# The down half of an MLP in 2x2 block products for two of three token groups

## The chip, the cores and the metric

One Trainium2 chip, one of its cores. The metric is the device time of one execution in microseconds; lower is better. The engines are PE (matrix products; PEld is its weight load), DVE (VectorE), ACT (ScalarE), POOL (GpSimd) and SP (SyncE), which here issues every data transfer.

## The reference, cut to what matters

Two layers over 1152 tokens (1024 of a prompt, 8 streams with 16 new ones each), model width 1024, inner width 4096:

```python
for l in range(DEPTH):                       # DEPTH = 2
    x = x + merge(attention parts of rmsnorm(x, norm1[l])) @ w_out[l]
    x = x + jnp.square(jax.nn.relu(rmsnorm(x, norm2[l]) @ w_up[l])) @ w_down[l]
y = rmsnorm(x, final_norm)
```

Everything is float32. The change is in the second line of the loop: `u = relu(h @ w_up)^2`, a matrix of 4096 by 1152, and `u @ w_down`.

## The kernel before, in words

**Layout and precision.** Activations lie feature by token: a tile has 128 features on the partitions and G = 384 tokens along the row, so there are NG = 3 token groups. A float32 operand is split in two halves of the type fp32r, a rounded value H (ACT) and the remainder L (`sub_l`, DVE or POOL). A product of two such operands is three matmuls: H by H, H by L, L by H. Each matmul is 128x128 weights against 128x384 values.

**Up stage.** For i from 0 to 15, two chunks (128 rows each) of `u` are made. `up_plain(i)` makes them directly: 3 groups, 2 chunks, 8 chunks of depth, 3 matmuls each. From i = 2, `up_seven(i)` (L1323) takes groups 0 and 1 as the two columns of a 2x2 block product: the weights' blocks are a11, a12, a21, a22 (two chunks of `u` by two halves of the depth), and seven block products in place of eight give the four results. The sums of weight blocks s1 to s4 are made for each i (L1328, L1329 on POOL, L1330, L1331 on DVE) and split again (`w_pair`, L1295: ACT copy, then DVE subtraction); the sums t1 to t4 of the activations were made once by `t_prep` (L1275) and stay in SBUF. The third group is done directly beside the seven products (`third`, L1339) for i below 14; for i = 14 and 15 it follows behind, in `up_plain(14, (2,))` and `up_plain(15, (2,))`. `put_u` (L1308) takes a result out of PSUM, squares it and stores it to DRAM.

**Down stage.** 8 blocks b of 4 chunks of `u` (512 rows). `load_u` (L1375) loads the 12 tiles of a block back and splits each in H (L154, ACT) and L (L138, DVE); they lie in the pool `h`, 48 slots of 128x384, which also holds the split input of the up stage. `down_block` (L1410) loops over 8 output chunks m: every second m it loads and splits 512 KB of weights (`w_raw`, `w_pair`), then, for each group, 4 chunks of depth by 3 matmuls run into one PSUM bank, and one DVE addition (L1424) adds it to `x`. The last block runs group after group, its weights loaded again for each, so that a group's final norm can start early.

**Order.** The program is traced in the order of the source and a list scheduler of the framework orders each engine's queue by priority and its own estimate of times; each engine then runs its queue in order and waits on semaphores. A tile of a pool takes a slot when an earlier tile of that pool is released by its last reader. SP's queue, too, runs in order: a transfer that waits for its slot or for its data holds what is queued behind it. The raw weight tiles `wr` have 2 slots, the split ones `wh`/`wl` 2 in one pool and every third pair in another.

Of the kernel before, what the change touches and what calls it, by code (L numbers as in the profile page):

```python
# [40 lines left out]
def body(ctx, tc, t):  # L41
# [84 lines left out]
    lmask = cpool.tile([P, 6, 64], F32, name="lmask")  # L126
    smask = cpool.tile([P, N_STREAM], F32, name="smask")
    fnorm = cpool.tile([P, KD], F32, name="fnorm")
    rm = cpool.tile([P, G + P], F32, name="rm")
    GP.memset(rm, 1.0)  # L130
    GP.memset(rm[:, 0:G].rearrange("p (n s) -> p n s", s=64)[:, :, 0:1], 0.0)
    GP.memset(rm[:, G:G + P].rearrange("p (n s) -> p n s", s=16)[:, :, 0:1], 0.0)
    cqbd = cpool.tile([P, N_STREAM, 32], F32, name="cqbd")
    GP.memset(cqbd.rearrange("p s k -> p (s k)"), 0.0)
# [5 lines left out]
    wextra, wturn = [None], [0]  # L140

# [57 lines left out]
    def norm_group(xs, gains, hs, g, pool=SQ_POOL):  # L199
        r = inv_rms([x[:, gsl(g)] for x in xs], 1024.0, pool=pool)  # L200
        for c in range(KD):
            hs[c].append((hpc("hH"), hpc("hL")))
            f = piece("hf")
            V.scalar_tensor_tensor(f, xs[c][:, gsl(g)], gains[:, c:c + 1], r, ALU.mult, ALU.mult)
            copy(hs[c][g][0], f)
            sub_l(V if c % 2 else GP, hs[c][g][1], f, hs[c][g][0])
        return r

    def raw_group(xs, gains, hs, g):

        for c in range(KD):
            hs[c].append((hpc("hH"), hpc("hL")))
            x = xs[c][:, gsl(g)]
            copy(hs[c][g][0], x, scale=gains[:, c:c + 1])
            V.scalar_tensor_tensor(hs[c][g][1], x, gains[:, c:c + 1], hs[c][g][0].bitcast(F32), ALU.mult, ALU.subtract)

# [17 lines left out]
    xs = [xpool.tile([P, NT], F32, name=nm("x")) for _ in range(KD)]  # L234
# [9 lines left out]
    for g in range(NG):  # L244
        for c in range(KD):
            load(xs[c][:, gsl(g)], t["x"][:, c, gsl(g)])
# [7 lines left out]
    load(lmask, t["lmask"])  # L254
# [3 lines left out]
    for l in range(DEPTH):  # L258
# [92 lines left out]
        if l > 0:  # L351
            for c in range(KD):
                store(t["xspill"][:, c, :], xs[c])
# [3 lines left out]
            ws = [load_first(l, i) for i in range(3)]  # L357
        def first_put(i, g, o):
# [211 lines left out]
        def ca_head(c, h, ap):  # L570
# [3 lines left out]
            for g in range(NG):  # L574
                lo, hi = g * G, min(NP_, (g + 1) * G)
                w = hi - lo
                for ci in (C_CQ, C_CK):
# [3 lines left out]
                    if ci == C_CQ:  # L581
                        copy(qH[:, lo:hi], f[:, 0:w])
                        sub_l(GP, qL[:, lo:hi], f[:, 0:w], qH[:, lo:hi])
                        if g == 2:
                            GP.tensor_copy(cqbd[hr, :, 16 * h:16 * h + 16],
# [25 lines left out]
        def ca_scores(c, box):  # L611
# [3 lines left out]
            for s0 in range(0, N_STREAM, 3):  # L615
                n = min(3, N_STREAM - s0)
                pt = bank("pv", "cass")
                for j in range(n):
                    mm(pt[r3, j * 144:(j + 1) * 144], cqbd[:, s0 + j, :], c.kc[:, s0 + j, :], start=True, stop=True)
# [94 lines left out]
        def gla_prep(p, g, gp):  # L714
# [20 lines left out]
            V.tensor_tensor_scan(u.b, rm[:, P:P + G] if g == 2 else rm[:, 0:G], la, 0.0, ALU.mult, ALU.add)  # L735
# [17 lines left out]
        def gla_levels(u, gp, mq):  # L753
            g = u.g
            for li, s in enumerate(LEVELS):
# [23 lines left out]
                mk = lmask[:, None, li, :].bitcast(U32).rearrange("p j (n s) -> p j n s", s=s)  # L779
# [97 lines left out]
        def gla_stream():  # L877
            with ExitStack() as stack:
                yield from gla_units(open_pool(stack, "gla"))
# [320 lines left out]
        def ca_stage():  # L1200
            with ExitStack() as outer:
                op = open_pool(outer, "cao")
                box = dict(scs=op.tile([96, N_STREAM, 144], F32, name=nm("scs")),
# [20 lines left out]
        xs = [xpool.tile([P, NT], F32, name=nm("x")) for _ in range(KD)]  # L1224
        banks(d=4, tp=2, pv=2)

        def out_last(gs):

            for m in range(KD):
                for g in gs:  # L1230
# [6 lines left out]
                    V.tensor_tensor(xs[m][:, gsl(g)], o, xo, ALU.add)  # L1237
# [23 lines left out]
        for g in range(NG):  # L1261
            with tc.high_priority(offset=100):
                raw_group(xs, gains, hs, g)
                rs.append(up.tile([P, G], F32, name=nm("rs")))
                copy(rs[g], inv_rms([x[:, gsl(g)] for x in xs], 1024.0))
                for c in range(KD):
                    store(t["xmid"][:, c, gsl(g)], xs[c][:, gsl(g)])
# [4 lines left out]
        def u_tile(s):  # L1272
            return up.tile([P, G], F32, tag="u", name=nm(s), bufs=5)

        def t_prep(j):  # L1275
            fs = []
            for c in (j, j + KH):
                for g in range(2):
                    f = tpool.tile([P, G], F32, tag="f", name=nm("f"), bufs=4)
# [3 lines left out]
            f11, f12, f21, f22 = fs  # L1283
# [5 lines left out]
            for n, f in ((2, t2), (3, t3), (1, t1), (4, t4)):  # L1289
# [3 lines left out]
                ts[n].append(o)  # L1293

# [13 lines left out]
        def put_u(ci, g, z):  # L1308
# [14 lines left out]
        def up_seven(i, rest):  # L1323
            raw = [w_raw(t["w_up"][l, 2 * i + c]) for c in range(2)]
            a11, a12, a21, a22 = (raw[x][:, y * KH:(y + 1) * KH, :] for x in range(2) for y in range(2))
            sa, sb = (tpool.tile([P, KD, P], F32, tag="ws", name=nm("ws"), bufs=2) for _ in range(2))
# [4 lines left out]
            V.tensor_tensor(s4, a12, s2, ALU.subtract)  # L1331

            def prod(o, w, half, x, first):
                for j in range(KH):
                    for k, (wi, ri) in enumerate(((0, 0), (0, 1), (1, 0))):
                        mm(o, w[wi][:, half * KH + j, :], x[j][ri], start=first and j == k == 0,
                           stop=j == KH - 1 and k == 2, skip_group_check=True)
# [21 lines left out]
            put_u(2 * i, 0, X)  # L1359
# [7 lines left out]
            put_u(2 * i + 1, 1, add("z22", Z, ec))  # L1367
# [3 lines left out]
            put_u(2 * i + 1, 0, add("z21", W, eb))  # L1371
            prod(Z, ws, 1, h2[1], False)
            put_u(2 * i, 1, add("z12", Z, eb))

        def load_u(b, pool, n):  # L1375
            us = []
            for q in range(4):
                row = []
                for g in range(NG):
# [187 lines left out]
```

## Time and profile before

| | |
|---|---|
| median of 3 runs | 3208.78 us (3202.6 to 3211.04) |
| the profiled execution | 3202.21 us, span 3200.4 us |
| granted TensorE clock, mean | 0.977 |
| busy share of the span | PE 95%, PEld 91%, DVE 62%, ACT 43%, POOL 25% |
| moved by DMA | 358.10 MB, mean 112 GB/s |

From the timeline of layer 0: the part with attention ends near 853 us, the up stage runs to about 1204 us, the down stage to about 1603 us; in layer 1 the same points lie at 2433, 2780 and 3187 us. A window's row gives its length, then each engine's busy time with the number of its instructions in brackets, then the granted clock, the share of DMA time and the rate in GB/s. A row of a group of instructions gives line, engine, operation, output and inputs, count, then busy time and the mean of one in ns, then the idle time ahead of it and what ended that.

### The profile page before, as it was taken

The numbers are of one execution on the slowest core, as the hardware profiler recorded it, in microseconds if no ns is written. First come the engines' busy times: TensorE is split into PE (matmuls) and PEld (weight loads), VectorE is DVE, ScalarE is ACT, GpSimd is POOL, SyncE is SP. The second block draws the span as 40 slices with busy tenths as digits, with TensorE's granted clock in tenths as the row PEclk, the third lists the DMA queues.
The fourth block names the chain that finished last, engine by engine and source line by source line (L and its number), as shares of the span: only waits on it lengthen the run. The fifth ranks groups of instructions, "written<-read, shape, count | busy, mean of one in ns | idle before, by whom it ended". The sixth has DMA issues, their size and how long they took to land.

```text
span 3200.4 us, 50248 instructions
## 1 busy us (share of the span) xinstructions
PE 3041.5 (95%) x18172; PEld 2911.2 (91%) x18172; DVE 1974.7 (62%) x3903; ACT 1371.0 (43%) x2995; POOL 811.4 (25%) x1010
## 2 busy tenths in 40 slices
PE   7999999988999999999999999989989999999998
PEld 7888887877999999999989898878879999999998
DVE  4665497885755565545555656978866555644446
ACT  4554354775533342212245544557754333412213
POOL 4332356552301110000153313554522111000002
PEclk9999899998999999999999999999999999999999
DMA  5333215224523245322343322142353223633313
GB/s 177 107 110 103 91 50 162 67 85 148 166 93 102 95 156 167 104 72 89 113 154 119 104 82 91 55 154 78 96 175 125 99 97 100 216 99 95 106 55 119
DMA packets 221144, 358.10 MB, mean 112 GB/s; under 512 B 27072, under 2 KB 185504, under 8 KB 220896
## 3 DMA queue, kind: packets, MB, share of 16 engines
q1 hardware_dynamic: 220896, 354.90, 34.6%
q8 instruction: 143, 2.34, 0.3%
q14 instruction: 105, 0.86, 0.1%
HBM read 251.77 MB, written 103.02 MB: 111 GB/s over the span
## 4 chain that ended last, share of the span: by engine, by line
PE 74%; DVE 11%; ACT 5%; DMA 4%; issue 3%; POOL 1%; SPq 1%; DVEq 0%; ACTq 0%; POOLq 0%
PE z L56 61%; PE pv L56 3%; PE s L56 2%; PE ptp L71 2%; DMA wr<-in_w_up_dram 1%; DMA cf<-zs_dram 1%; ACT P L427 1%; PE lev L56 1%; PE glao L56 1%; DVE ng L422 1%; SPq L74 1%; DVE ga L780 1%; PE rb L56 1%; DVE sbd L833 1%; DVE mq L771 1%
## 5 line engine op out<-in xcount | busy, mean ns | idle before, releaser
L56 PE MATMUL z<-uH,wdn 128*128 128x384 f32 x3072 | 781.7, 334 | 0.0
L56 PEld LDWEIGHTS z<-uH,wdn 128*128 128x128 f32 x3072 | 554.4, 188 | 0.0
L56 PE MATMUL z<-uL,wdn 128*128 128x384 f32 x1536 | 513.5, 334 | 0.0
L56 PE MATMUL z<-hH,wup 128*128 128x384 f32 x1728 | 451.8, 336 | 6.9 <-DVE u L1311 5.5
L1424 DVE TENSOR_TENSOR x<-z,x 128x384 f32<-128x384 f32 x336 | 186.9, 556 | 315.8 <-PE z L56 314.5
L56 PEld LDWEIGHTS z<-hH,wup 128*128 128x128 f32 x1728 | 314.7, 189 | 9.1 <-DVE u L1311 6.1
L1299 ACT ACTIVATE wdn<-wr 128x1024 fp32r<-128x1024 f32 x80 | 84.7, 1059 | 487.4 <-PE z L56 483.8
L56 PE MATMUL z<-hL,wup 128*128 128x384 f32 x864 | 290.4, 336 | 0.0
L56 PEld LDWEIGHTS z<-uL,wdn 128*128 128x128 f32 x1536 | 288.3, 188 | 0.0
L169 POOL TENSOR_TENSOR sq<-x 128x384 f32<-128x384 f32 x28 | 29.6, 1058 | 894.9 <-DVE x L1424 797.9
L1312 ACT ACTIVATE u<-u 128x384 f32<-128x384 f32 x192 | 100.0, 521 | 280.3 <-DVE u L1311 276.3
L1311 DVE SCALAR_TENSOR_TENSOR u<-z,rs 128x384 f32<-128x384 f32 x192 | 106.5, 555 | 156.9 <-PE z L56 155.0
L427 ACT ACTIVATE P<-s,ng 128x320 f32<-128x320 f32 (+5 forms) x288 | 157.7, 552 | 99.9 <-DVE ng L424 63.5
L1328 POOL TENSOR_TENSOR ws<-wr 128x512 f32<-128x512 f32 x28 | 46.3, 1653 | 537.7 <-DMA wr<-in_w_up_dram 440.2
L56 PE MATMUL z<-ts,wus 128*128 128x384 f32 x1008 | 180.5, 335 | 0.8 <-ACT wus L1299 0.8
L138 DVE TENSOR_TENSOR PT<-ptp,PT 128x512 fp32r<-128x512 f32 (+3 forms) x288 | 146.4, 516 | 52.9 <-ACT PT L154 44.6
L154 ACT ACTIVATE PT<-ptp 128x512 fp32r<-128x512 f32 (+3 forms) x288 | 128.6, 461 | 115.3 <-PE ptp L71 114.1
L56 PEld LDWEIGHTS z<-ts,wus 128*128 128x128 f32 x1008 | 174.9, 188 | 1.6 <-ACT wus L1299 1.4
L56 PEld LDWEIGHTS z<-hL,wup 128*128 128x128 f32 x864 | 163.2, 189 | 0.0
L71 PE MATMUL ptp<-ident,P 128*128 128x128 f32 x792 | 140.3, 282 | 18.4 <-DVE PT L138 6.8
L422 DVE TENSOR_REDUCE ng<-s 128x1 f32<-128x320 f32 (+5 forms) x288 | 146.5, 515 | 5.9 <-PE s L56 2.7
L154 ACT ACTIVATE uH<-ur 128x384 fp32r<-128x384 f32 x192 | 97.1, 523 | 100.7 <-PE z L56 80.1
(440 smaller groups left out, 7269.8 us busy)
## 6 DMA issues: line engine op xcount, KB each, us to landing
wr<-in_w_down_dram SPq DMA_DIRECT2D x80, 512.0 KB, 3.3
wr<-in_w_up_dram SPq DMA_DIRECT2D x72, 512.0 KB, 3.8
u_dram<-u SPq DMA_DIRECT2D x192, 192.0 KB, 1.9
ur<-u_dram SPq DMA_DIRECT2D x192, 192.0 KB, 3.5
zs_dram<-z SPq DMA_DIRECT2D x102, 192.0 KB, 1.9
wo1r<-in_w_out_dram SPq DMA_DIRECT2D x48, 320.0 KB, 3.0
cf<-zs_dram SPq DMA_DIRECT2D x144, 96.0 KB, 2.5
of<-os_dram SPq DMA_DIRECT2D x48, 192.0 KB, 3.4
```

What stands on the lines that cost most here:

```text
L56: i = T.matmul(*a, **k).ins
L71: T.transpose(out, in_, idn)
L74: nc.sync.dma_start(dst, src)
L138: eng.tensor_tensor(lo, src, h.bitcast(F32), ALU.subtract)
L154: S.activation(o, i, AF.Copy, scale=scale)
L422: V.tensor_reduce(ng[:, x:x + 1], sc[x][:, :hi - lo], AX.X, ALU.max, negate=True)
L427: S.activation(pr[:, lo:hi], sc[x][:, :hi - lo], AF.Exp, bias=ng[:, 0:1], accum_out=ss[:, x:x + 1])
L1299: S.activation(h, raw, AF.Copy)
L1311: V.scalar_tensor_tensor(u, z, 0.0, rs[g], ALU.max, ALU.mult)
L1312: S.activation(u, u, AF.Square)
L1328: GP.tensor_tensor(s1, a21, a22, ALU.add)
L1424: V.tensor_tensor(x, o, x if xo is None else xo, ALU.add)
```

## The change

- **Down in seven products.** `u` for groups 0 and 1 is multiplied with `w_down` in 2x2 block products: two output chunks (m, n = m + 1) by two halves of a block of 8 chunks of `u` (1024 rows; 4 blocks in place of 8), seven block products of 12 matmuls each in place of eight (`down_seven`). One common term of three results is summed over the blocks in `eb` and added at the end. Weight sums are made per pair of output chunks with the same function as in the up stage (`w_sums`), on POOL and DVE, and split again.
- **Sums of `u` in the up stage.** For each i, `u_sums` makes t1 to t4 of the four results (3 additions on DVE, 1 on POOL), splits each (4 ACT copies, 4 DVE subtractions) and stores H and L to a new DRAM tensor `td`: 8 stores of 192 KB. One of the six stores of `u` falls away (it isn't read again). For i = 0 and 1, whose `u` came from `up_plain`, the four tiles are loaded again and summed at i = 3 and 4. For this `put_u` writes into tiles `f` (4 slots), `u` has 2 slots in place of 5, `td` 6.
- **Operands of a block.** `load_block` brings 12 raw tiles (split on arrival as before) and 16 sums as 32 stored halves without any work of an engine: 56 tiles of 128x384 in 48 slots of `h` and 20 of a new pool, 5 of each 17 there.
- **Third group alone.** After the four blocks, the third group runs by itself: 4 blocks, 8 output chunks, 24 matmuls for each 512 KB of weights, which are loaded and split a second time.
- **Moved.** `lmask`, `rm` and `cqbd` move from the constants into the pools of their stages (loaded or set once a layer); `x` is kept as a tile for two groups and one for the third; the stores of `x` between the layers go ahead of the third group's pass for groups 0 and 1, and behind the first weight loads of layer 1 for the third.

```diff
         def put_u(ci, g, z, keep=False):
-            u = u_tile("u")
+            u = f_tile("u") if keep else up.tile([P, G], F32, tag="u", name=nm("u"), bufs=2)
             V.scalar_tensor_tensor(u, z, 0.0, rs[g], ALU.max, ALU.mult)
             S.activation(u, u, AF.Square)
-            store(t["u"][l, ci, :, gsl(g)], u)
+            if not (keep and g == 1 and ci % 2 == 0):
+                store(t["u"][l, ci, :, gsl(g)], u)
+            return u
...
+        def u_sums(i, fs=None):
...
+            for n, f in sums(*fs):
+                h, lo = (up.tile([P, G], F32R, tag="td", name=nm("td"), bufs=6) for _ in range(2))
+                copy(h, f)
+                sub_l(V, lo, f, h)
+                store(t["td"][l, i, n - 1, 0], h.bitcast(F32))
+                store(t["td"][l, i, n - 1, 1], lo.bitcast(F32))
...
+            return blk(0, 0), sm_(1), sm_(3), blk(1, 0), blk(1, 1), sm_(2), sm_(4)
...
+        def down_seven(b, p, ops):
+            b11, t1, t3, b21, b22, t2, t4 = ops
+            m, n = 2 * p, 2 * p + 1
+            raw = [w_raw(t["w_down"][l, b, m + c]) for c in range(2)]
+            sa, sb = w_sums(raw, dpool)
+            X, Y, W, Z = (bank("d", "z")[:, :G] for _ in range(4))
+            w0 = w_pair(raw[0], "wdn")
+            prod(X, w0, 0, b11, True)
+            if b == 0:
+                copy(eb[p], X)
+            else:
+                V.tensor_tensor(eb[p], X, eb[p], ALU.add)
+            wb = w_pair(sb, "wds")
+            prod(Z, wb, 0, t1, True)
+            acc(n, 1, Z, b == 0)
+            wa = w_pair(sa, "wds")
+            prod(W, wa, 1, t3, True)
+            acc(n, 1, W, False)
+            prod(X, w0, 1, b21, False)
+            acc(m, 0, X, b == 0)
+            prod(Z, wb, 1, b22, False)
+            acc(m, 1, Z, b == 0)
+            prod(Y, wa, 0, t2, True)
+            V.tensor_tensor(eb[p], Y, eb[p], ALU.add)
+            h, lo = (dpool.tile([P, KH, P], F32R, tag=x, name=nm("wd")) for x in ("w1h", "w1l"))
+            S.activation(h, raw[1][:, KH:, :], AF.Copy)
+            sub_l(V, lo, raw[1][:, KH:, :], h)
+            prod(W, (h, lo), 0, t4, False)
+            acc(n, 0, W, b == 0)
+            if b == 3:
+                for x in (xs[n][1], xs[m][1], xs[n][0]):
+                    V.tensor_tensor(x, x, eb[p], ALU.add)
...
         up_plain(14, (2,))
-        us = load_u(0, tpool, 4)
+        ops = load_block(0)
         up_plain(15, (2,))
...
+        for b in range(4):
+            if b:
+                ops = load_block(b)
+            for p in range(KH):
+                down_seven(b, p, ops)
+        us = load_third(0, rpool, 4)
...
+        for b in range(4):
+            if b:
+                us = load_third(b, dn, 6)
             for m in range(KD):
+                w = w_pair(w_raw(t["w_down"][l, b, m]), "wdn")
+                o = bank("d", "z")[:, :G]
+                dense(o, w, lambda k: us[k], KD)
+                acc(m, 2, o, b == 0)
```

More of the change, by code (lines that the diff above doesn't have):

```diff
@@ L357, in body @@
             ws = [load_first(l, i) for i in range(3)]
+            for c in range(KD):
+                store(t["xspill"][:, c, gsl(2)], xs[c][2])
         def first_put(i, g, o):
@@ L1270, in body, with f_tile, sums @@
         ts = [[] for _ in range(5)]
[L1272 to L1279, printed above, removed]
[L1280 to L1283 removed]
+        def f_tile(s):
+            return tpool.tile([P, G], F32, tag="f", name=nm(s), bufs=4)
+        def sums(f11, f12, f21, f22):
             t1, t2, t3, t4 = (piece("t") for _ in range(4))
@@ L1331, in up_seven, with prod @@
             V.tensor_tensor(s4, a12, s2, ALU.subtract)
[L1333 to L1337, printed above, removed]
+            return sa, sb
+        def prod(o, w, half, x, first):
+            for j in range(KH):
+                for k, (wi, ri) in enumerate(((0, 0), (0, 1), (1, 0))):
+                    mm(o, w[wi][:, half * KH + j, :], x[j][ri], start=first and j == k == 0,
+                       stop=j == KH - 1 and k == 2, skip_group_check=True)
+        def up_seven(i, rest):
+            raw = [w_raw(t["w_up"][l, 2 * i + c]) for c in range(2)]
+            sa, sb = w_sums(raw, tpool)
             def third(w, c):
@@ new lines, in load_raw, with load_block, blk, sm_ @@
+        def load_raw(src, pool, n, tile_):
+            r = pool.tile([P, G], F32, tag="f", name=nm("ur"), bufs=n)
+            load(r, src)
+            o = tile_("uH"), tile_("uL")
+            copy(o[0], r)
+            sub_l(V, o[1], r, o[0])
+            return o
+        def load_block(b):
+            def blk(c, g):
+                return [load_raw(t["u"][l, KD * b + 2 * j + c, :, gsl(g)], rpool, 4, d_tile) for j in range(KH)]
+            def sm_(n):
+                row = []
+                for j in range(KH):
+                    o = d_tile("tH"), d_tile("tL")
+                    for y in range(2):
+                        load(o[y].bitcast(F32), t["td"][l, KH * b + j, n - 1, y])
+                    row.append(o)
+                return row
+            return blk(0, 0), sm_(1), sm_(3), blk(1, 0), blk(1, 1), sm_(2), sm_(4)
@@ new lines, in load_third, with acc @@
+        def load_third(b, pool, n):
+            return [load_raw(t["u"][l, KD * b + 2 * j + c, :, gsl(2)], pool, n, hpc)
+                    for c in range(2) for j in range(KH)]
+        def acc(m, g, o, first):
+            x = xs[m][g]
+            if first:
+                xo = piece("xo")
+                load(xo, t["xmid"][:, m, gsl(g)])
+                V.tensor_tensor(x, o, xo, ALU.add)
+            else:
+                V.tensor_tensor(x, o, x, ALU.add)
+        def down_seven(b, p, ops):
[8 more added lines that the diff above has]
+                copy(eb[p], X)
+            else:
+                V.tensor_tensor(eb[p], X, eb[p], ALU.add)
[19 more added lines that the diff above has]
+                    V.tensor_tensor(x, x, eb[p], ALU.add)
@@ L1408, in body @@
+        us = load_third(0, rpool, 4)
+        dstack.close()
+        if l < DEPTH - 1:
+            for c in range(KD):
+                for g in range(2):
+                    store(t["xspill"][:, c, gsl(g)], xs[c][g])
+        for x, y in zip(xs, x_tiles(open_pool(xstack, "xt", "right"), range(1))):
+            x += y
+        banks(d=6, nm=2)
         dn = open_pool(ustack, "dn")
-        def down_block(us, b, gs):
+        wextra[0], wturn[0] = dn, 0
+        for b in range(4):
+            if b:
+                us = load_third(b, dn, 6)
```

151 lines of the change are left out of this document (73 added, 78 removed).

## The prediction

> **What bounds the kernel now.** I read the page first (engines, groups), then the chain of work that ended last, then windows over the stages, then the timeline of SP and ACT around a block of the down stage.
>
> ```profile
> span 3200.4 us, 50248 instructions
> PE 3041.5 (95%) x18172; PEld 2911.2 (91%) x18172; DVE 1974.7 (62%) x3903; ACT 1371.0 (43%) x2995; POOL 811.4 (25%) x1010
> L56 PE MATMUL z<-uH,wdn 128*128 128x384 f32 x3072 | 781.7, 334 | 0.0
> L56 PE MATMUL z<-uL,wdn 128*128 128x384 f32 x1536 | 513.5, 334 | 0.0
> ```
>
> PE is busy for 95%, and the products of the down stage (3072 + 1536 = 4608, 2304 a layer) have 0.0 us idle ahead of them. A mean of 334 ns is not their price, since matmuls overlap. The price is the distance from one to the next, which the chain and the windows give:
>
> ```profile
> 853.04 311.76 PE z L56 x1788
> 1184.11 5.69 DMA wr<-in_w_up_dram
> 1191.79 5.39 DMA wr<-in_w_up_dram
> 1199.66 391.16 PE z L56 x2255
> ```
>
> ```profile
> 853.00:1165.00 312.00, 311.75 (x1788) 311.43 (x1788) 176.47 (x235) 107.88 (x160) 40.06 (x27) 1.00 0.32 103
> 1165.00:1204.00 39.00, 37.26 (x207) 35.61 (x208) 29.60 (x45) 21.10 (x37) 2.80 (x2) 1.00 0.72 237
> 1204.00:1400.00 196.00, 196.00 (x1133) 196.00 (x1132) 93.00 (x157) 40.98 (x63) 0.00 (x0) 1.00 0.35 114
> 1540.00:1603.00 63.00, 63.00 (x376) 63.00 (x375) 37.50 (x57) 21.77 (x32) 10.32 (x9) 1.00 0.40 139
> 2741.00:2780.00 39.00, 37.29 (x209) 35.72 (x208) 29.40 (x43) 20.02 (x32) 2.90 (x2) 1.00 0.67 224
> ```
>
> The chain follows PE alone for 312 us of the up stage and 391 us of the down stage; between them weight loads are on it. The third row: 196 us for 1133 matmuls at a granted clock of 1.00, 0.173 us each, PE never idle, DVE at 47%. The two rows of 39 us are the end of the up stage (i = 14 and 15 and their third group): 207 and 209 matmuls are worth 35.8 and 36.2 us, so 3 us are lost in each layer, with DVE at 76% and DMA at 0.72 and 0.67. These rows are the nearest to the new down stage: seven products without a third group, much DVE, much DMA.
>
> **The change, part by part.**
>
> *Matmuls.* Per layer, groups 0 and 1 took 8 blocks x 8 chunks x 2 groups x 12 = 1536; now 4 x 4 pairs x 7 x 12 = 1344. The third group keeps 768. So 192 fall away a layer, 384 in all, x 0.173 = **-66.4 us**, since nothing else had its end there. All else is cost.
>
> *Work of the other engines.* The prices:
>
> ```profile
> L1328 POOL TENSOR_TENSOR ws<-wr 128x512 f32<-128x512 f32 x28 | 46.3, 1653 | 537.7 <-DMA wr<-in_w_up_dram 440.2 <-DVE wup L138 56.7 <-DVE z L1347 40.5
> L1329 POOL TENSOR_TENSOR ws<-wr,wr 128x512 f32<-128x512 f32 x28 | 38.5, 1376 | 0.0
> L1330 DVE TENSOR_TENSOR ws<-ws,wr 128x512 f32<-128x512 f32 x28 | 47.7, 1704 | 21.2 <-POOL ws L1328 21.2
> L1331 DVE TENSOR_TENSOR ws<-wr,ws 128x512 f32<-128x512 f32 x28 | 19.0, 678 | 0.0
> L1347 DVE TENSOR_TENSOR z<-z,eb 128x384 f32<-128x384 f32 x56 | 31.0, 554 | 35.9 <-PE z L56 35.9
> L138 DVE TENSOR_TENSOR wdn<-wr,wdn 128x1024 fp32r<-128x1024 f32 x80 | 100.7, 1259 | 24.8 <-ACT wdn L1299 24.7
> L138 DVE TENSOR_TENSOR uL<-ur,uH 128x384 fp32r<-128x384 f32 x192 | 100.6, 553 | 19.3 <-ACT uH L154 18.8 <-PE z L56 0.3
> L138 DVE TENSOR_TENSOR ts<-t,ts 128x384 fp32r<-128x384 f32 x32 | 23.1, 745 | 0.2
> L1299 ACT ACTIVATE wdn<-wr 128x1024 fp32r<-128x1024 f32 x80 | 84.7, 1059 | 487.4 <-PE z L56 483.8 <-DMA wr<-in_w_down_dram 3.5
> L154 ACT ACTIVATE uH<-ur 128x384 fp32r<-128x384 f32 x192 | 97.1, 523 | 100.7 <-PE z L56 80.1 <-DMA ur<-u_dram 20.2
> ```
>
> *Up stage, i = 2 to 13.* Each i has 132 matmuls, 22.9 us. `u_sums` adds 3 additions (0.55) and 4 subtractions (0.55 to 0.745) on DVE, 3.9 to 4.6 us; 4 ACT copies, 2.1 us; one POOL addition; 7 more transfers net. DVE goes from 57% (176.47 of 312) to about 75%, ACT from 35% to 44%; both stay below PE. What can leak is order: on SP a td store waits for a late subtraction and the next i's weights stand behind it. Lower bound 0 (the gapless row), upper bound the loss rate of the 39 us rows, 8% of 275 us. The weights are loaded most of an i ahead and the gapless row is the same code, so I take 1.5 us a layer: **+3**.
>
> *i = 14 to the first block.* In 39 us DVE was busy 29.6; two or three `u_sums` fall in it (about 4.3 each) and the first `w_sums` (1.70 + 0.68): 40.6 to 45, more than the window. DVE becomes the longest queue there by 2 to 6 us. Beside it `load_block(0)` brings 12 raw tiles as before and 32 stored halves more, 44 of 192 KB = 8.65 MB against 2.36:
>
> ```profile
> wr<-in_w_down_dram SPq DMA_DIRECT2D x80, 512.0 KB, 3.3
> ur<-u_dram SPq DMA_DIRECT2D x192, 192.0 KB, 3.5
> 1185.00:1215.00 30.00, 29.36 (x168) 28.68 (x167) 19.32 (x31) 14.60 (x25) 0.00 (x0) 1.00 1.00 340
> ```
>
> At the 340 GB/s at which this window is already full, 6.3 MB more are 18.5 us. Slots come free from the first products of i = 15 on, so most of it lies under 31 us of matmuls and under the first pair, which needs its operands one product (2.08 us) after another. Also the first `w_sums` writes where `up`'s tiles lay and waits for the last of them. Bounds 0 and 18.5 a layer, I take 5, near the DVE overshoot: **+10**.
>
> *Down in seven.* A pair p has 84 matmuls, 14.5 us; 16 pairs a layer, 233 us. DVE per pair: sums 1.70 + 0.68, splits 3.5 x 1.26 = 4.41, seven additions from PSUM 3.89, a quarter of 12 raw splits 1.66: 12.3 us, 85%. ACT 3.5 x 1.06 + 3 x 0.52 = 5.3; POOL 3.0. DMA per block of 58.2 us: 8 x 0.524 + 8.65 = 12.8 MB, 221 GB/s. All below PE on average, but in the fourth pair DVE has most of the 12 raw splits on top of 10.7 us. How far ahead loads go is seen here:
>
> ```profile
> 1247.83 3.13 ACT L154 ACTIVATE uH<-ur 128x384 fp32r<-128x384 f32 x6 [5.70 <-PE z L56]
> 1248.98 6.53 SPq L74 DMA_DIRECT2D ur<-u_dram  x10
> ```
>
> Before, the splits for a coming block start 5.7 us ahead of the end of a block, when its last output chunk begins to release slots. Now a block takes 56 of 68 slots, so 12 are free early and the other 44 follow in the last pair, product by product, each needed 7 products (14.5 us) later. These are 28 stored halves and 8 raw tiles: 7.1 MB from t = 2 us of the last pair on, with about 1.5 MB of weights between, are 25 us at 340 GB/s and end at 27 us, when the last operand is due (14.5 + 12.5 = 27). It just fits. The split of w0 for the next pair starts when product 4 ends and leaves 3.5 us of slack; those of wb and wa as much. Lower bound 0; upper bound the rate of the 39 us rows, 8% of 233 = 18.6 us a layer. I take 7 a layer, since DVE stands above that row's 76% but three of four pairs have little DMA: **+14**.
>
> By the Trainium skill, "SBUF — State Buffer", section "Who interferes with whom", a DVE instruction with two SBUF inputs and a POOL instruction that reads SBUF block each other for a whole instruction. The trace agrees: 1704 ns beside POOL's second sum, 678 ns for the same shape without. By that rule another subtraction that meets a POOL sum waits up to 1.4 us more, DVE stands at 13.7 of 14.5 us in each pair, and the sum would go with the upper bound, 12 us more a layer, 3191 us: the second rival below.
>
> *Third group alone.* 32 weights a layer, each for 24 matmuls, 4.16 us. The last block before had that shape: the window 1540 to 1603 has PE 63.00 of 63. Opening new pools and PSUM banks between the passes, and the norms, may cost or (norms of groups 0 and 1 now 133 us early, weights ahead of the `x` stores) gain; bounds -3 to +5 a layer, I take 1: **+2**.
>
> *Moved constants.* A load, three memsets on POOL at the start of a stage, twice; they precede work that waits for other loads. Bounds -3 and +6 in all, taken 0.
>
> **Sum.** 3202.2 - 66.4 + 3 + 10 + 14 + 2 = 3164.8 by the profiled execution. The median shown is 6.6 us above that execution and the fastest run equals it; I add half: **3168 us**.
>
> **The rivals.**
>
> *All hidden.* Every cost lands in idle time of DVE, ACT and DMA, as in the gapless rows: 3202.2 - 66.4 = 3136, with half the run difference 3139. For it: DVE below 100% in each stage but one. Against: the 39 us rows lose 3 us each at a lower load.
>
> *DVE and the weights bind in the down pairs.* Splits in order behind raw splits and additions, and POOL's blocking, take all 3.5 us of slack: the upper bounds of the rows, 2 x 18.6 in the pairs and 2 x 11 at the transition, give 3202 - 66 + 37 + 22 + 5 + 3 = 3203 at worst, 3185 half way. For it: 85%; against: PSUM's 8 banks hold two pairs.
>
> *Slower: the operand burst starves PE at each block.* Place: the first pair of the 8 blocks. SP takes transfers in order; if a td load that waits for its slot stands ahead of `wr` loads, or the burst starts only when the last pair ends, its 7.1 MB (21 us) and the weights behind lie open but for what the first pair covers. The loss is then up to 15 us a block, 8 x 15 = 120, 3168 - 14 + 120 = 3274; at 8 us a block it is 3218. It decides from 8 us a block on (66 us lost in 8 blocks cancels the gain). Against: the two rows above show loads started as slots come free.
> By the Trainium skill, "TensorE: Matmul & The Clock Gate", section "HAM oscillation — how this bites in real kernels", such waits, beyond about 3.4 us, would halve the clock for as long after them; that would add up to 1.7 us to each wait, 14 us in all. No stage quoted here shows it, their clock is 1.00.
>
> *No change.* The upper costs of two parts together, 3200 to 3218.
>
> **How the numbers follow.** 0.3% of this time, about 10 us, is what a measurement can tell from no change. Forecast (3148 to 3185) 0.48; all hidden 0.22; DVE and weights (3185 to 3199) 0.13: together faster 0.83. Same 0.08. Slower 0.09. The range goes from 3138 (all hidden) to 3202 (upper bounds of the pairs and the transition); about 0.04 lies below and 0.14 above.
>
> **What would show it.** Right: 4224 matmuls in the down stage, 0.173 us apart, seven-pass pairs of 14.5 to 15.5 us, the third pass gapless with 24 matmuls per weight pair. Wrong: PE waiting on DMA into operand tiles in the first pair of a block (the burst); PE waiting on `wds` splits in every pair with DVE near 100% (the second rival); an up stage longer than 24 us per i.

## The result: 1.6% slower

The changed kernel takes 3261.23 us (median of 4 runs, 3255.27 to 3263.1) against 3208.75 us: ratio 1.0163, 95% interval [1.0144, 1.0183]. The forecast was 3168 us; 384 matmuls fewer made the kernel 52 us slower. The page after, its engines, the costliest product of the new stage and three of the DMA rows:

```profile
span 3261.3 us, 51233 instructions
PE 3021.3 (93%) x17788; PEld 2875.2 (88%) x17788; DVE 2241.7 (69%) x4191; ACT 1510.6 (46%) x3211; POOL 940.8 (29%) x1110
...
DMA packets 297906, 475.57 MB, mean 146 GB/s; under 512 B 35600, under 2 KB 257136, under 8 KB 297648
...
L56 PE MATMUL z<-tH,wds 128*128 128x384 f32 x768 | 221.0, 358 | 46.5 <-ACT wds L1324 38.2 <-DMA tL<-td_dram 4.5 <-DMA tH<-td_dram 3.8
...
wr<-in_w_down_dram SPq DMA_DIRECT2D x128, 512.0 KB, 3.7
td_dram<-td SPq DMA_DIRECT2D x256, 192.0 KB, 2.1
ur<-u_dram SPq DMA_DIRECT2D x160, 192.0 KB, 4.7
```

The 384 matmuls are gone (18172 to 17788), but the products of the sums wait 46.5 us, mostly for the split of the summed weights (`wds`). Moved bytes rose from 358.10 to 475.57 MB. By stage, windows over layer 0 (length, then busy time of PE, PEld, DVE, ACT, POOL with counts, granted clock, DMA share, GB/s):

```profile
818.00:922.00 104.00, 99.62 (x584) 98.21 (x583) 69.92 (x112) 48.23 (x91) 21.51 (x16) 1.00 0.36 118
922.00:976.00 54.00, 49.95 (x281) 48.05 (x280) 42.60 (x60) 21.62 (x36) 12.21 (x8) 1.00 0.65 217
976.00:1169.00 193.00, 193.00 (x1115) 193.00 (x1114) 149.00 (x211) 80.96 (x133) 33.20 (x25) 1.00 0.49 165
1169.00:1220.00 51.00, 42.70 (x219) 40.42 (x218) 36.30 (x52) 21.57 (x35) 7.80 (x6) 0.93 0.71 232
1220.00:1280.00 60.00, 48.29 (x228) 45.92 (x228) 35.00 (x47) 18.77 (x27) 8.55 (x6) 0.83 0.73 249
1299.00:1501.00 202.00, 183.11 (x997) 179.64 (x996) 141.07 (x203) 62.90 (x86) 33.52 (x24) 0.97 0.55 186
1468.00:1624.00 156.00, 155.84 (x901) 155.64 (x900) 92.51 (x130) 55.75 (x74) 7.74 (x6) 1.00 0.53 169
1212.00:1230.00 18.00, 11.92 (x42) 10.90 (x43) 9.75 (x14) 7.38 (x13) 2.49 (x2) 0.72 1.04 361
```

A window holds as many matmuls as its length over 0.1734 us if PE never waits. The third row is full (1115 in 193 us), with DVE at 77%. The second, where the first two slices' sums are read back, lacks 5 us; the fourth and fifth, from the end of the up stage into block 0, lack 13.0 and 20.5 us. The last row shows why: DMA is full at 361 GB/s, PE gets 42 matmuls in 18 us, and the clock falls to 0.72. From the timeline, the last matmul of layer 0's up stage is at 1209.3, and the fourth and the last of the 16 pairs end at 1299.3 and 1501.6: block 0 takes 90.0 us and blocks 1 to 3 202.3 us, where pairs of 14.7 us would make 58.8 and 176.4. The third pass takes 136.6 (768 matmuls: 133.2). SP's queue at the two places (start, duration, transfer, count):

```profile
1205.54 4.26 SPq L77 DMA_DIRECT2D td_dram<-td  x7
1209.89 1.84 SPq L74 DMA_DIRECT2D ur<-u_dram  x4
...
1214.45 0.92 SPq L74 DMA_DIRECT2D tH<-td_dram  x2
...
1354.74 0.33 SPq L74 DMA_DIRECT2D wr<-in_w_down_dram  x1
1355.30 8.10 SPq L74 DMA_DIRECT2D ur<-u_dram  x5
...
1372.15 0.81 SPq L74 DMA_DIRECT2D wr<-in_w_down_dram  x2
```

Block 0's first operand is requested at 1209.89, after the last matmul of the up stage. In the 15 us before, SP waited 4.6 us for DVE to split weights of the up stage and 2.9 us for ACT and DVE to finish what it stores; the seven stores of sums just ahead take 4.26 us, most of it for issuing them. From 1209.9 to 1219 no wait of SP is longer than 0.3 us, so their place in the queue held the loads, not their slots. An earlier place in the 14 us before would have given little, though, as the DMA share ahead of that request and behind it shows:

```profile
1195.50:1209.90 14.40, 14.18 (x82) 13.86 (x80) 10.96 (x18) 6.77 (x11) 1.64 (x1) 1.00 0.80 259
1209.90:1236.00 26.10, 13.95 (x52) 12.42 (x52) 15.51 (x20) 9.76 (x17) 5.95 (x4) 0.78 1.01 350
```

In the 14.4 us before, a share of 0.20 was free, 3 us of transfers by estimate; behind it DMA is full for 26 us. In the last pair of block 1, between a weight load at 1354.74 and the next two at 1372.15, stand five `ur` and 16 `td` loads; the `ur` row alone takes 8.10 us, since its fifth load waits until the first of the four raw slots has been filled and split. What PE and SP then wait for, 1200 to 1470 (engine and line, what, total us, times, longest):

```profile
PE z L56 <- ACT wds L1324: 15.0, 6, 3.0
PE z L56 <- ACT uH L148: 7.8, 2, 4.0
PE z L56 <- DMA tL<-td_dram: 4.5, 1, 4.5
...
SPq L74 <- DVE wdn L131: 45.6, 6, 15.3
SPq L74 <- PE z L56: 19.9, 24, 4.8
```

The summed weights of a pair go through the raw loads, two sums on POOL and two on DVE, the ACT copy and the DVE subtraction before PE can use them. SP waits 45.6 us for DVE to release a raw weight slot (the `wdn` split).

### The profile page after: what moved, and what is told of

Read it like the earlier page. It is cut to its first block, busy times and chain, and to the rows that moved or that the text cites. A ratio compares the mean times of both kernels' runs of the same rounds, so it can differ in the third digit from the quotient of the medians.

```text
span 3261.3 us, 51233 instructions
## 1 busy us (share of the span) xinstructions
PE 3021.3 (93%) x17788; PEld 2875.2 (88%) x17788; DVE 2241.7 (69%) x4191; ACT 1510.6 (46%) x3211; POOL 940.8 (29%) x1110
## 2 busy tenths in 40 slices
DMA packets 297906, 475.57 MB, mean 146 GB/s; under 512 B 35600, under 2 KB 257136, under 8 KB 297648
## 4 chain that ended last, share of the span: by engine, by line
PE 63%; DVE 15%; DMA 9%; ACT 6%; issue 4%; SPq 2%; POOL 1%; DVEq 0%; ACTq 0%; POOLq 0%
PE z L56 50%; PE pv L56 3%; PE s L56 2%; DMA wr<-in_w_down_dram 2%; PE ptp L71 2%; SPq L74 1%; DMA tH<-td_dram 1%; DVE ws L1357 1%; DMA ur<-u_dram 1%; DMA wr<-in_w_up_dram 1%; ACT P L425 1%; DMA cf<-zs_dram 1%; PE glao L56 1%; DVE ng L420 1%; DVE ga L778 1%
## 5 line engine op out<-in xcount | busy, mean ns | idle before, releaser
L56 PE MATMUL z<-uH,wdn 128*128 128x384 f32 x1536 | 409.6, 340 | 10.5 <-ACT uH L148 8.4
L1355 POOL TENSOR_TENSOR ws<-wr 128x512 f32<-128x512 f32 x60 | 84.2, 1403 | 761.8 <-DMA wr<-in_w_down_dram 403.1
L56 PEld LDWEIGHTS z<-uH,wdn 128*128 128x128 f32 x1536 | 283.0, 191 | 12.1 <-ACT uH L148 9.4
L56 PE MATMUL z<-tH,wds 128*128 128x384 f32 x768 | 221.0, 358 | 46.5 <-ACT wds L1324 38.2
L56 PE MATMUL z<-uL,wdn 128*128 128x384 f32 x768 | 260.8, 340 | 0.7 <-DVE uL L131 0.6
L1324 ACT ACTIVATE wdn<-wr 128x1024 fp32r<-128x1024 f32 x96 | 101.6, 1059 | 275.4 <-PE z L56 240.4
L56 PEld LDWEIGHTS z<-tH,wds 128*128 128x128 f32 x768 | 150.1, 201 | 54.1 <-ACT wds L1324 47.3
L1469 DVE TENSOR_TENSOR x<-z,x 128x384 f32<-128x384 f32 x176 | 97.1, 553 | 128.8 <-PE z L56 127.4
L56 PEld LDWEIGHTS z<-uL,wdn 128*128 128x128 f32 x768 | 146.3, 191 | 2.0 <-DVE uL L131 1.9
L131 DVE TENSOR_TENSOR wdn<-wr,wdn 128x1024 fp32r<-128x1024 f32 x96 | 121.5, 1265 | 36.7 <-ACT wdn L1324 36.7
```

The lines of the kernel that those rows point to most:

```text
L56: i = T.matmul(*a, **k).ins
L131: eng.tensor_tensor(lo, src, h.bitcast(F32), ALU.subtract)
L1324: S.activation(h, raw, AF.Copy)
L1355: GP.tensor_tensor(s1, a21, a22, ALU.add)
L1469: V.tensor_tensor(x, o, x, ALU.add)
```

## The experiments

The time outside the MLP stages varies between kernels that are alike there by some 20 us, so each trace's *MLP time* is given too: from the first matmul of the up stage to the last of the down stage, both layers added. In the kernel before, the first matmul of the up stage is at 818.9 us in layer 0 and 2396.0 in layer 1, earlier than the 853 and 2433 at which its timeline was divided above.

| | us, median | ratio to before, 95% | MLP time |
|---|---|---|---|
| before | 3208.75 to 3212.41 | | 1578.1 |
| after | 3261.23 | 1.0163 [1.0144, 1.0183] | 1638.9 |
| x1_up_only | 3229.68 | 1.0062 [1.0044, 1.008] | 1596.2 |
| x2_td_once | 3222.46 | 1.003 [1.0012, 1.0049] | 1587.1 |
| x3_wr4 | 3224.59 | 1.0047 [1.0031, 1.0064] | 1588.6 |
| x4_early0 | 3260.06 | 1.0155 [1.013, 1.018] | 1631.5 |
| x5_third_first | 3237.49 | 1.0085 [1.0062, 1.0108] | 1570.2 |
| x6_third_first_wr4 | 3229.29 | 1.0063 [1.0041, 1.0085] | 1558.9 |
| x7_direct | 3228.11 | 1.0058 [1.004, 1.0075] | 1549.1 |
| x8_wr4_pool | 3226.3 | 1.0045 [1.0028, 1.0062] | 1600.0 |
| x9_split | 3204.54 | 0.999 [0.9969, 1.001] | 1569.1 |
| x10_split_only | 3225.34 | 1.0055 [1.0034, 1.0077] | 1595.5 |
| x11_cover | 3196.7 | 0.9953 [0.9931, 0.9975] | 1565.3 |
| x12_one | 3206.2 | 0.9989 [0.9971, 1.0008] | 1570.7 |
| x13_late_sums | 3197.08 | 0.9969 [0.9953, 0.9985] | 1567.0 |
| x14_late_sums_rest | 3220.1 | 1.0033 [1.0016, 1.0051] | 1581.1 |
| x15_xo_late | 3212.88 | 1.0008 [0.9991, 1.0025] | 1585.0 |
| x16_split_wr4 | 3209.54 | 0.9998 [0.9981, 1.0016] | 1575.9 |

### The parts: x1 to x4

**x1: the up stage's sums alone**, with the old down stage.

```diff
-            if not (keep and g == 1 and ci % 2 == 0):
-                store(t["u"][l, ci, :, gsl(g)], u)
+            store(t["u"][l, ci, :, gsl(g)], u)
...
-        (down_seven and its loads)
+        (down_block and load_u of the kernel before)
```

> The up stage of the changed kernel (sums of u made, split and stored, all stores of u kept) with the down stage of the kernel before: the cost of the sums alone. Theory 1 (the loss lies in the down stage's transfers): about 6 us a layer, as the changed kernel's up stage shows, so 3208.8 + 12 = 3221 us (3214 to 3232). Rival (the sums overload VectorE and SyncE's queue and this is the main loss): 3208.8 + 50 or more.

The sums cost 20 us, not the few us forecast: MLP time +18, of which the up stage 2.8 us a layer (387.3 against 384.5 in layer 0) and the down stage's start 5.9 (408.5 against 402.6).

**x2: the sums' operands loaded only for block 0** (blocks 1 to 3 multiply block 0's sums).

```diff
+            if b == 0: held = t1, t3, t2, t4 = sm_(1), sm_(3), sm_(2), sm_(4)
+            else: t1, t3, t2, t4 = held
```

> The changed kernel, but the sums of u are loaded for the first block alone and used again for blocks 1 to 3 (their values are left out there): 32 of the 44 operand loads of each later block fall away, bytes, slots and queue places together; all matmuls, weight sums and additions stay. Theory 1 and theory 2 (both: the burst of operand loads at the start of a block): the 27 us a layer that blocks 1 to 3 lose go, 3261 - 54 = 3207 us (3195 to 3220). Rival (VectorE at 85% and the chain of weight sums hold each pair): stays within 10 us of 3261.

**x3: four raw weight slots in the pairs in place of two.**

```diff
-            raw = [w_raw(t["w_down"][l, b, m + c]) for c in range(2)]
+            raw = [w_raw(...m), dpool.tile([P, KD, P], F32, tag="wr", bufs=2)]
+            load(raw[1], t["w_down"][l, b, n])
...
-        eb = [dpool.tile(...) for _ in range(KH)]
+        eb = [piece("eb") for _ in range(KH)]
```

> The changed kernel with 4 slots for the raw weights of the seven-product pairs in place of 2 (eb moves to the pool of pieces, the raw operand tiles have 3 slots in place of 4). Theory 1 (the weights of the second and third pair come late, since their loads can start only when a slot of two comes free and then stand behind the operands' burst): most of the first pairs' loss in blocks 1 to 3 goes, 3261 - 30 to 50 = 3211 to 3231 us. Theory 2 (the bytes of the burst are the limit, whichever transfer is late): at most 10 us less, 3251 to 3261.

Blocks 1 to 3, x2 and then x3:

```profile
1289.00:1467.00 178.00, 176.03 (x1001) 174.98 (x1000) 134.53 (x196) 57.47 (x80) 30.05 (x24) 1.00 0.37 116
```

```profile
1297.00:1480.00 183.00, 179.60 (x1013) 178.32 (x1012) 143.68 (x205) 63.99 (x90) 33.16 (x24) 0.99 0.64 212
1212.00:1230.00 18.00, 5.89 (x18) 4.47 (x18) 3.68 (x8) 4.10 (x8) 0.00 (x0) 0.69 1.00 333
```

From 202.3 us to 177.6 (x2) and 182.5 (x3). x3 carries all the bytes (212 GB/s) and loses 6 us where the changed kernel lost 26: the loss is the weights' late start, not the bytes by themselves. Both remedies cure most of it, since it needs both the row of `td` loads on SP and the two slots. Block 0 keeps its loss in both (89.5 and 85.5 us): in x3, 18 us with 18 matmuls.

**x4: 24 of block 0's operand tiles requested before the last slices of the up stage.**

```diff
+        ops = block_a(0)      # b11 and the sums 1 and 3, in slots of h
         tstack.close()
...
-        ops = load_block(0)
+        ops += block_b(0)
```

> The changed kernel with the first 24 operand tiles of block 0 allocated from the large pool only and requested before the pools of the up stage are closed, so that their loads can start while the last products of the up stage run (the other 20 slots take the last 20 tiles of each block). Theory 1 (block 0's 32 us a layer are lost because its loads start only when the up stage has ended): 15 to 25 us a layer come back, 3211 to 3231 us. Rival (the transfers are at their limit there, earlier requests only push others): within 10 us of 3261.

Block 0 got shorter by 12.4 us (90.0 to 77.6), but the up stage longer by 4.5, where those loads now stood ahead of its weights, and blocks 1 to 3 longer by 5 us. Gain moved, not made.

### Block 0: more notice, x5 to x8

**x5: the third group's pass before the pairs**, so that its 133 us cover block 0's loads. **x6** is x5 with x3's slots; **x7** is x6 with the first two slices' sums made from tiles at hand.

```diff
+        for b in range(4):
+            (third group, block b)        # moved up; result stored to xmid
+            if b >= 2: parts += load_block(0, b - 2)
         for b in range(4):
             ... down_seven(b, p, ops)
-        (third group's pass)
+        load(x[2], t["xmid"][:, c, gsl(2)])
```

> The changed kernel with one thing moved: the third group's pass of the down product (256 matmuls... some 133 us of gapless PE a layer) stands before the four blocks instead of behind them, its result waits in DRAM, and block 0's operands are requested in its second half. Two raw weight slots as in the changed kernel. Theory A (block 0 loses its 32 us a layer, and the end of the up stage 5 more, because 11 MB of operands, the old x and the weights are all requested within a few us at the end of the up stage): with 60 us of notice the first two pairs end 30 to 32 us after the third pass, not 54.6; 3261 - 2 x 28 = 3205 us. Theory B (the loss is the weights' own path through two raw slots, whatever the operands do): block 0 still loses over 20 us a layer, 3245 us or more. The new stage boundary itself (third pass to pairs) is priced at 2 to 4 us a layer by either.

> As x5_third_first, with four raw weight slots as in x3_wr4 (3224.6 us). Theory A: the two losses add up and so do the two cures: 3225 - 2 x 26 = 3172 us, faster than the kernel before by about 1.1%, and block 0 runs at 14.7 us a pair. Theory B: with four slots block 0 had already what it could get; 3215 us or more.

> As x6_third_first_wr4, and the sums of the first two slices of 256 rows are made from the up stage's tiles while these are at hand, instead of being read back from DRAM after slices 3 and 4 through the four slots that the running slices also use (where the changed kernel lost 5.4 us a layer in 54). Theory A (the four slots): 5 us a layer less, 3162 us. Rival (DVE and ACT are what is short, and the stage's first slices have less of them left): the loss moves to the first slices and the time stays at that of x6 within 4 us.

Block 0, then blocks 1 to 3, then the end of the program in x5:

```profile
1337.00:1400.00 63.00, 62.82 (x359) 62.23 (x358) 43.81 (x56) 20.02 (x27) 11.36 (x8) 1.00 0.59 191
1400.00:1595.00 195.00, 184.93 (x1018) 181.88 (x1017) 139.55 (x198) 62.57 (x84) 36.03 (x26) 0.97 0.56 186
3194.00:3229.00 35.00, 11.80 (x53) 11.05 (x52) 21.00 (x39) 11.44 (x27) 17.18 (x17) 0.54 0.46 166
```

Theory A was right on block 0's pairs and wrong on the total. Block 0's pairs now run near the full pitch, though 9.5 us (x5) and 16.9 us (x6) are still lost between the last up product and the end of block 0, where the changed kernel lost 31: in x5 the third pass now waits 3.9 us for its own first operand. MLP time falls from 1638.9 to 1570.2, 1558.9 (x6) and 1549.1 us (x7), 29 below the kernel before. But with all three groups ending in the last pairs, 36 us follow the last product instead of the changed kernel's 13, and the way to the next up stage takes 813.2 us instead of 790.8: about 45 us come back. (What x9's expectation says of x7, 820.4 and 40.4 us, leaves out the pairs' last products; from the very last one it is 815.3 and 35.3.) At the layer's end some 10 of the 22 are seen in the first 30 us, where PE gets 120 matmuls in place of 177; the rest is spread over the next stage and wasn't located. x5, x6 and x7 also deal the operands to their slots in another order, and so do x9 to x14 and x16; what this alone does was not run.

**x8: x3 with the pairs' weights requested by POOL's queue, a pair ahead.**

```diff
+                nc.gpsimd.dma_start(r[c], t["w_down"][l, k // 4, k % 4 * 2 + c])
```

> x3_wr4 (four raw weight slots, 3224.6 us) with the down weights of the pairs requested by POOL's queue, one pair ahead, instead of SP's; nothing else moved. Theory R1 (the weights are late because SP's one queue puts them behind the operand loads that wait for their slots): block 0's weights come 15 us earlier and it loses 8 to 12 us a layer instead of 27, the starts of blocks 1 to 3 lose 0 to 2 instead of 6: 3225 - 2 x 20 = 3185 us. Theory R2 (it is the bytes: all 16 engines are full for 30 us and the weights share them whichever queue asks): 3215 to 3230 us, with the weights' landing times at 8 to 12 us a load.

```profile
1211.00:1294.00 83.00, 69.81 (x338) 63.72 (x337) 52.58 (x72) 28.01 (x41) 21.74 (x22) 0.86 0.84 278
1212.00:1230.00 18.00, 7.24 (x18) 4.62 (x17) 7.20 (x9) 5.10 (x8) 6.69 (x7) 0.60 0.99 327
```

PE still gets 18 matmuls in those 18 us. The first pair's weights were asked for at 1200.33 and 1203.33 and landed at 1204.72 and 1207.31, before the last up product; in x3, with SP, they landed at 1204.68 and 1208.02. So the first pair's raw weights did not come late in either, and R1 falls for them. What PE waits for from 1211 to 1260, and what POOL does ahead of the first weight sum (L1355):

```profile
PE z L56 <- ACT uH L148: 6.5, 6, 3.0
PE z L56 <- ACT wds L1324: 5.7, 1, 5.7
```

```profile
1212.32 0.57 POOL L1475 DMA_DIRECT2D wr<-in_w_down_dram  x1 [7.42 <-DVE u L1336]
1221.24 0.53 POOL L1475 DMA_DIRECT2D wr<-in_w_down_dram  x1 [8.35 <-DMA tL<-td_dram]
1221.78 1.27 POOL L1355 TENSOR_TENSOR ws<-wr 128x512 f32<-128x512 f32 x1
```

The longest wait is for the split of that sum. POOL's queue goes on 0.03 us after each of the last two `u` stores of the up stage has landed (1220.08 and 1220.58; the row names another transfer), and in the changed kernel, too, POOL's first sum, at 1216.99, follows such a landing, at 1216.37. This fits the wait that the prediction names, for the last of the up stage's tiles. The other waits are for the split of operands that arrive at the rate of a full DMA. So x8 shows that a second queue brings no more bytes (327 GB/s, 333 in x3); what each of the two waits is worth, it doesn't.

### Notice before, cover behind: x9 to x12

**x9: x7 with two blocks of the third pass before the pairs and two behind. x10: the changed kernel with that alone. x11: x9 with the third group's share of slices 12 and 13 also done at the end of the up stage. x12: x9 with one block before, three behind.**

```diff
+        for b in range(FIRST):            # 2; in x12 1
+            third_pass(b, us[b], ...)     # block 0's loads between its chunks
         ... pairs ...
-        for b in range(4):
+        for b in range(FIRST, 4):         # continues from xmid
...
-            up_seven(i, i < 14)
+            up_seven(i, i < 12)           # x11 alone, and up_plain(12, (2,)), up_plain(13, (2,))
```

> x7_direct with the third group's pass cut in two: two of its four blocks (66 us a layer) before the pairs, its partial sum stored to DRAM, two after them. In x5 to x7 the time came back elsewhere: with the third pass first, the last pairs end all three groups at once, and the next layer's first norm (or the last one) stands bare: 820.4 us from the down stage to the next up stage instead of 790.8, and 40.4 us behind the last pair instead of 13.3. Theory A' (operands hidden before, norms hidden behind: both need some 60 us of other work): x7's profiled span 3222.8 - 29.6 - 26.8 + 3 a layer for one more boundary = 3172 us, median within 8 of it, faster than the kernel before by about 1%. Rival (66 us behind the pairs do not cover the norms of two groups, or the partial sum's way through DRAM costs as much as it saves): 3200 us or more.

> The changed kernel with the third pass cut in two as in x9_split and nothing else: two raw weight slots, the first two slices' sums read back from DRAM. This prices block 0's start alone. Theory A': the 32 us a layer that block 0 lost shrink to about 6, so 3261 - 2 x 26 + 2 x 3 = 3215 us; if the blocks 1 to 3 run as in x5 (17 us a layer lost instead of 27, from the operand tiles' new order of slots) 3190 to 3200. Rival (block 0's loss is not a matter of notice): 3245 or more.

> x9_split, with the third group's share of the up slices 12 and 13 also done at the end of the up stage (four slices of one group, 33 us, instead of two, 17 us) and the first third-group operands of the down stage requested before them. In x7 the 40 us from the end of the up stage on hold 143 of 234 matmuls, some 15 us lost. Theory A': 33 us of cover are enough, 8 to 12 us a layer come back, 4 more weight loads cost nothing: 3150 to 3158 us. Rival (what is late there is DVE's and ACT's work on the last slices' sums, which moves along): within 5 us of x9.

> x9_split with one block of the third pass before the pairs (33 us) and three behind: how much notice do block 0's operands need? If it is bytes (7 MB of operands behind the third pass's own, at 340 GB/s some 20 us), 33 us are enough and the time is that of x9 within 6 us, or better by what the norms still lack. If it is SP's order and the slots, 32 of the 56 tiles can be asked for only when the pass ends: the first block loses 10 to 20 us a layer against x9, 3190 to 3210 us.

The third pass's first two blocks with the notice alone (x10; two stretches of 20 us, which hold 115 matmuls at full pitch), then blocks 1 to 3:

```profile
1208.00:1228.00 20.00, 15.07 (x75) 14.08 (x74) 9.47 (x15) 8.99 (x15) 0.00 (x0) 0.91 0.94 318
1248.00:1268.00 20.00, 14.78 (x72) 13.96 (x72) 9.37 (x14) 6.69 (x12) 0.00 (x0) 0.83 0.99 348
1351.00:1546.00 195.00, 183.00 (x1011) 181.01 (x1010) 148.11 (x208) 65.21 (x90) 36.39 (x25) 0.97 0.59 197
```

x10 gains as much as x3, 36 us, but only a part of it at block 0. Its pairs there follow at 14.1 to 14.7 us, yet from the last up product to the end of block 0 143.1 us pass, where 384 matmuls of the third pass (66.6) and four pairs (58.8) make 125.4. So 18 of the 31 us are still lost, now in the third pass, where DMA is nearly full. The rest comes from blocks 1 to 3, which take 194.8 us in place of 202.3 in layer 0 and 192.8 in place of 203.8 in layer 1. In x9 the costs behind the pairs are gone (788.5 us from the last product of the down stage to the next up stage), but it came out at 3204.5, 32 us above the forecast of 3172; up to the end of block 0 it still loses 21 us. x11, with more cover, is faster than the kernel before by 0.47%, the fastest here, though some 40 us above its forecast. One block of notice (33 us) is as good as two (66 us): x12 is within 2 us of x9, and it too still loses 22 us up to the end of block 0. x11, with 17 us more work of the up stage behind the last sums, loses 8 there, but its up stage takes 397.5 us in place of x9's 386.8.

### What is left: x13 to x16

**x13: x11 with the pairs' blocks in the order 1, 2, 3, 0, and the first two slices' sums made during the third pass. x14: x13 without x11's edit. x15: x3 with the old `x` added in block 2, not loaded in block 0. x16: x3 and x10 together.**

```diff
+        SEQ = (1, 2, 3, 0)                # x13, x14
+                if m == 5: u_sums(b)      # in the third pass
...
-                xo = piece("xo"); load(xo, ...); V.tensor_tensor(x, o, xo, ALU.add)
+                copy(x, o)                # x15, groups 0 and 1; xo added at b == 2
```

> x11_cover with the four blocks of pairs taken in the order 1, 2, 3, 0 and the sums of the first two slices (needed by block 0 alone) read back and made in the first half of the third group's pass, where DVE is busy for half the time, not in the up stage. In x11 the gaps between matmuls longer than 0.3 us add up to 38.5 us in layer 0's MLP (before: 16.4), 8.4 of them at 877 to 917, where these sums are made. Theory S (DVE's and ACT's work in the wrong place): these 8 us a layer come back, 3197 - 16 = 3181 us. Rival (something else in the first slices, the sums t of the activations, has the gaps): within 5 us of x11.

> x13_late_sums with the third group's share of slices 12 and 13 put back beside their seven products (only 14 and 15 done behind, as in the changed kernel). Slices without the third group lost 1.6 to 3.2 us each in x11 (1117 to 1200), but behind them the down stage's operands were covered. Theory S2 (a slice of seven products alone is too short for its weights' way through two raw slots; cover behind is worth more): 3 to 10 us slower than x13. Rival: equal, the one loss for the other.

> x3_wr4 (3224.6 us) with the old x (16 tiles of 192 KB a layer, 3.1 MB) not loaded in block 0 but added in block 2; ACT copies the first partial results instead. In x3 block 0's first pairs still lose 27 us a layer with DMA 1.00 busy at 333 GB/s for 18 us. Theory bytes: 3.1 of some 13 MB fall out of the burst, 9 us of transfers at that rate, of which those ahead of the second pair's end count, some 4 to 8 us a layer: 3209 to 3217 us. Theory order (the operands' slots and the stores ahead of them on SP set the start; the old x comes behind the operands anyway): 3222 to 3227 us.

> The changed kernel with both cures and nothing else: four raw weight slots (alone: 3224.6 us, -37) and the third pass cut in two (alone: 3225.3, -36). If they are separate losses in separate places they add up: 3261 - 73 = 3188 us. If they cure in part the same waits (the weights stand behind the operands in the first pairs of block 0 as in the others): 3200 to 3210 us, as x9 gave with one edit more.

x11, then x13, the place of the first slices' sums and the third pass:

```profile
877.00:917.00 40.00, 35.21 (x182) 33.80 (x181) 27.25 (x41) 18.47 (x33) 6.65 (x5) 0.91 0.39 132
1240.00:1310.00 70.00, 66.30 (x369) 64.73 (x368) 43.99 (x56) 23.78 (x33) 8.80 (x5) 0.98 0.87 293
```

```profile
877.00:917.00 40.00, 40.00 (x233) 40.00 (x232) 25.84 (x35) 13.52 (x22) 6.59 (x5) 1.00 0.36 117
1240.00:1310.00 70.00, 63.49 (x345) 62.13 (x346) 43.61 (x58) 23.69 (x33) 7.46 (x5) 0.95 0.92 314
```

Theory S was right about the place: 233 matmuls in place of 182. About half of it (24 matmuls, 4 us) is lost again in the third pass, where DMA goes from 0.87 to 0.92, and the time does not move. x14 is 23 us slower than x13 (MLP time 14): the slices without a third group are worth their loss. x15 is 12 us faster than x3 by the medians, as theory bytes said, but its trace does not show it in block 0: from the last up matmul to the end of the fourth pair 83.4 us against 85.5 in layer 0, 86.1 against 86.9 in layer 1. Of the 18.5 us between the two traces 3.7 are MLP time, so most of it lies in stages that the edit leaves alone, and theory bytes is not shown. x16 shows that the two cures overlap: 52 us in place of 73. Both shorten blocks 1 to 3, and together they do it hardly more than x3 alone: 181.1 us in layer 0, against 182.5 in x3 and 194.8 in x10.

## Why the prediction was wrong, step by step

- **Matmuls, -66.4 us: right.** 384 fewer; undisturbed pairs take 14.7 us (14.5 forecast).
- **Up stage, +3: measured +7**, 6.5 us in layer 0 (391.0 against 384.5) and 0.9 in layer 1. The slices in the middle are gapless, as forecast. The loss in layer 0 is where the first two slices' sums are read back (5 us) and at the last slices; neither was costed.
- **i = 14 to the first block, +10: this term failed most.** Block 0 lost 31 us a layer, +62. The sentence that failed is "Slots come free from the first products of i = 15 on, so most of it lies under 31 us of matmuls": the first operand was requested at 1209.89, when those matmuls were over, behind weights and stores in SP's queue, and DMA had a share of only 0.20 free in the 14 us before. The prediction counted DVE's overshoot there, but not SP's queue and not what DMA already carried; and it left out the 16 loads of the old `x`, 3.1 MB, in the same block, which x15 moves away for 2.1 and 0.8 us. The wait of the first weight sum for the last of the up stage's tiles, which the term names, came true: POOL starts it at 1216.99, 7.7 us after the last up product. The upper bound of 18.5 us was the time of the added bytes alone. What was right is the rate (340 GB/s; 327 to 361 in the 18 us rows above). That more work ahead of block 0 shrinks the loss was shown by x5 (31 to 9.5 us) and x10 (to 18); how much of it is the queue's order and how much the bytes at one place was not run apart, and x4, which only asks earlier, gained 12 us there and lost most of it before and behind.
- **Down in seven, +14: measured 26 and 27 us in the two layers beyond block 0, +53.** "It just fits" was the step: it let 25 us of loads end at 27 us and gave the weights 1.5 MB among them, but not a place in the queue. With two raw slots, a weight load that waits behind them makes the whole chain of sum, split and product late: block 2's first two pairs take 19.2 and 22.6 us in layer 0. x2 and x3 show it. The upper bound of 18.6 us a layer, a loss rate taken from rows of another stage, was too low as well.
- **Third group alone, +2: nothing.** It takes 3.4 and 4.7 us more than its 768 matmuls, but the kernel before has the same short matmuls of the norms there, and its down stage takes 3.1 and 4.5 us more than its 2304 (402.6 and 404.0 against 399.5). The bound of 3 us on what its place is worth was too low: with the pass elsewhere 45 us come back (x5).
- **The sum.** -66 + 7 + 62 + 53 = 56 of the 61 us by which MLP time grew; most of the rest is 32 pairs at 14.7 us in place of 14.57, the time of their matmuls.
- **The range.** Its upper end, 3202, rests on 11 us a layer for the transition, where the term's own bound was 18.5; with that it would be 3218. The time lies above this too.
- **The rivals.** "The operand burst starves PE at each block", given 0.09, is what happened, with the mechanism named there (a `td` load ahead of `wr`). Its price was 15 us for each of 8 blocks and its threshold 8; measured are 31 for two blocks and about 9 for six, 115 in all. That this is near the 120 of that sum is luck, since no block lost what it said. "DVE and the weights bind in the pairs" is refuted: in x2, DVE is busy 134.53 of 178 us, 76%, and 9 of the 12 pairs in layer 0 follow at 14.7.
- **The two rules.** From the Trainium skill's section "Who interferes with whom" (SBUF — State Buffer), by which DVE and POOL block each other, the prediction worked out up to 12 us a layer. The trace has the blocking: the DVE sum that meets POOL's second sum takes up to 1.79 us against 0.68 without.

```profile
L1357 DVE TENSOR_TENSOR ws<-ws,wr x60: 677/1772/1792, 864.7 to 3089.2; 128x512 f32<-128x512 f32 x60
```

  In the undisturbed pairs of x2, where that row is the same within 4 ns, a pair takes at most 0.2 us more than its matmuls, so it did not decide. From the Trainium skill's section "HAM oscillation — how this bites in real kernels" (TensorE: Matmul & The Clock Gate) the prediction took up to 1.7 us for each wait; the trace agrees that the clock halves, as the rows below show. What it cost beside the waits was not measured apart.

## What to carry to other kernels

A stage that saves matmuls by loading more must be costed by when its first load can be *issued* (which slot it waits for, and what waits ahead of it in the issuing queue) and by what DMA already carries in the time that is to cover it. A sum of bytes over a rate that ends just in time leaves nothing for a chain behind it (here weights with two slots): two slots more were worth 37 us. Moving another pass in front was worth 36 us, but the pass that now comes first lost part of what block 0 had lost. When a pass is moved to give cover, look at what it covered before.

## What was not expected of the hardware

The clock answers to short waits. Three windows of the changed kernel at block 0's start:

```profile
1218.00:1221.00 3.00, 0.00 (x0) 0.00 (x0) 2.42 (x2) 1.13 (x2) 1.48 (x2) 0.98 1.04 357
1221.00:1224.00 3.00, 1.76 (x5) 1.45 (x6) 2.72 (x3) 1.60 (x3) 0.00 (x0) 0.50 1.07 381
1224.00:1227.00 3.00, 3.00 (x10) 3.00 (x10) 0.10 (x1) 0.04 (x1) 0.00 (x0) 0.50 1.05 363
```

After 4.5 us of idle time (1217.8 to 1222.2), PE is busy for the whole of the third window and does 10 matmuls where 17 go at full clock. And DMA gave 357 to 381 GB/s to one core over these 9 us, more than the 340 that the forecast took as full.
